# A decoder trunk on one core: first loads reordered, more warm-up matmuls, one PSUM tile moved, the last LayerNorm regrouped

## The chip, the core and the metric

The kernel runs on one core of one Trainium2 chip. The metric is the device time of one execution in microseconds (us). Beside it stands a profiled execution, whose trace gives the start and length of every instruction on five engines: TensorE (PE for matmuls, PEld for the weight loads that go ahead of them), VectorE (DVE), ScalarE (ACT), GpSimd (POOL) and SyncE (SP), and of the transfers on the core's 16 DMA engines.

## What is computed

One sequence of 256 tokens with 2048 features goes through two layers, all in float32:

```
for layer in (0, 1):
    shift, scale, gate = split(silu(c) @ ada_w[layer] + ada_b[layer], 3)
    h = x * (1 + scale) + shift
    y = ssd_mixer(h) if layer == 0 else dilated_attention(h, k, v)
    x = layer_norm(alpha * x + (1 + gate) * y) * ln_g[layer] + ln_b[layer]
    if layer == 0:
        k, v = split(x @ kv_w, 2)
```

The SSD mixer projects `h` to a gate z, to xs, B, C and dt, puts xs, B and C through a causal convolution of width 4, and forms for each of 8 groups a masked score matrix of C and B. The scores, weighted by decays, are multiplied with xs. The second layer is attention in three groups with dilated windows. The last step is a LayerNorm over 2048 features, times `ln_g`, plus `ln_b`.

## The kernel before

**Splitting.** Every large product runs in three passes. A weight piece `raw` (128 partitions x 1024 floats) is split by `split` (L97) into `whi`, a rounded copy made by ACT (L100), and `wlo`, the rest, made by DVE (L102); the activations are split in the same way. TensorE multiplies high by high, high by low and low by high (L151 to 153, L190 to 193, L224, L232 to 234).

**Order.** The program is written against a tile framework. It derives the semaphores from the data, and a list scheduler sets the order on each engine; `tc.issue_after` holds an instruction behind another one. An engine works its list strictly in order. A transfer uses one of eight semaphores in turn, so the ninth transfer waits at its issuing queue until the first has landed, and what stands behind it on that queue waits too.

**The start (L451 to 630).** `c` arrives as the small block `crow`; six warm-up matmuls of ones (`warm`, L457, two instructions each) run meanwhile. DVE splits `crow` (L466, L467), TensorE spreads it over all partitions in four tiles `cps` (L473), ACT makes silu(c) of each, `cb_` (L476), and 14 more warm-up matmuls follow. The shift and scale of a block of 128 features are each a dot product over a 1 MB block `araw` of `ada_w`: `fetch` (L483, through L310) loads one, DVE works it off in 2.3 us (L317; the first is cut in two halves, L501 and L503). From shift, scale and x^T (`xt`, loaded by `fetch_x`, L488) ACT makes `htmp` (L522) and `actT` (L524). The first three weight pieces come in half pieces (`begin_piece`, L558, and `end_piece`, L562); their first halves are multiplied unsplit (`plain`, L567, L575). The first loads are issued at L71 and L590 to L601, all on SP's queue but three: `c`, the bias block `adab` and the first `xt` go out on ACT's queue.

**The first SSD group.** `stage1(g)` (L739) multiplies B and C into the scores `pcb`, in a tile of the pool `aux`. That pool has two PSUM buffers, given out in turn; a buffer is handed on when its last reader is done. DVE masks the scores and copies them out (L748, L749). TensorE then transposes xs (L770) twice, for b = 0 and b = 1, each time into another `aux` tile; DVE makes `xd`, `y` and `xo` of them (L772, L775, L780). `stage2(g)` (L787) multiplies the weighted scores with `xd` into `py` (L803, pool `aux2`, also two buffers) and `cb` with `xo` into `po` (L792, `aux`). Meanwhile TensorE works on the products of the next group.

**The end (L1274 to 1346).** The block b = 1 is normalised last. Its mean comes from `bn_aggr` (L1289). For the column chunks 0 to 2, TensorE forms `u - mean * ln_g` in PSUM: `plus` (L1321) multiplies `u` by the identity, `centre` (L1325) adds `diag` times `ln_g`, where `diag` is the identity times minus the mean, made by DVE (L1328). Chunk 3 is centred by DVE itself (L1329). Meanwhile ACT takes a square root (L1290) and DVE refines the inverse root `r1` (L1293 to 1296). At last DVE multiplies each chunk by `r1` and adds `ln_b` (L1344), and SP stores it (L1272).

Of the kernel before, what the change touches and what calls it, by code (L numbers as in the profile page):

```python
# [9 lines left out]
F32 = mybir.dt.float32  # L10
# [3 lines left out]
ALU = mybir.AluOpType  # L14
# [35 lines left out]
def trunk(ctx, tc, xT, x, c, par, cst, bias, lnrow, ada, wdt, win, wxs, wout, wk, wv, wbin, wbout, out):  # L50
# [305 lines left out]
    with ExitStack() as cA:  # L356
# [15 lines left out]
        with ExitStack() as cS:  # L372
# [78 lines left out]
            with ExitStack() as c0:  # L451
# [9 lines left out]
                    return after  # L461

                at = mm.tile([P, 2, L], F32, name="acc")
                last = warm(6, at)
                crow2 = pe.tile([48, P + KT], F32R, name="crow", bufs=1)
                V.tensor_copy(crow2, crow)  # L466
                V.tensor_tensor(crow2[32:, :P], crow[32:, :P], crow2[32:, :P].bitcast(F32), op=ALU.subtract)  # L467
                with tc.tile_pool(name="ec", bufs=4, space=PSUM) as ec:
                    for n in range(4):
                        cps = ec.tile([P, 512], F32, name="cps")  # L470
                        for j in range(4):
                            with tc.issue_after(last.ins):
                                last = T.matmul(cps[:, j * P:j * P + P],  # L473
                                                crow2[:, P + 4 * n + j:P + 4 * n + j + 1].to_broadcast([48, P]),
                                                crow2[:, :P], start=True, stop=True)
                        S.activation(cb_[:, 512 * n:512 * n + 512], cps, AF.Silu)  # L476
                    last = warm(14, at, last)
                ex = c0.enter_context(tc.tile_pool(name="ex", bufs=4, space=PSUM))
                first = [acc_pair(ex), acc_pair(ex)]
                cols = [(0, kind, kt) for kt in range(KT) for kind in ("scale", "shift")]  # L480
# [2 lines left out]
                def fetch():  # L483
                    i = len(raws)
                    if i < len(cols):
                        raws.append(ada_load((wp1, pe)[i // 2 % 2], *cols[i]))

                def fetch_x(kt):  # L488
                    xts[kt // 2] = pe.tile([P, 2, L], F32, name="xt")
                    (nc.sync if kt else nc.scalar).dma_start(xts[kt // 2], xT[:, kt:kt + 2, :])  # L490

                def h_step():

# [94 lines left out]
                    halves[i] = [t.rearrange("p (k n) -> p k n", k=2) for t in halves[i]]  # L588

                nc.scalar.dma_start(adab_, par[:, :NB])  # L590
                fetch_x(0)
                fetch()
                fetch()
                begin_piece(0)
                begin_piece(1)
                fetch()
                fetch()
                begin_piece(2)
                for i in range(3):
# [139 lines left out]
            def stage1(g):  # L739

                pcb = aux.tile([P, 512], F32, name="aux")[:, :384].rearrange("p (a n) -> p a n", a=3)
                bm, cm_ = bc[g][:, 0, :], bc[g][:, 1, :]
                T.matmul(pcb[:, 0:3:2, :], bm[:, 0:P], cm_, start=True, stop=True)
                T.matmul(pcb[:, 1, :], bm[:, P:L], cm_[:, P:L], start=True, stop=True)
                cb = px.tile([P, 3, P], F32, name="cb")
                V.tensor_tensor(cb[:, 0:2, :], pcb[:, 0:2, :], tri[:, None, :].to_broadcast([P, 2, P]), op=ALU.mult)  # L748
                V.tensor_copy(cb[:, 2, :], pcb[:, 2, :])  # L749
                segs = []  # L750
                for w in range(2):
                    h0 = g * HPG + 4 * w
                    cbc = px.tile([P, 4, 2, P], F32, name="cbc")
                    nc.sync.dma_start(cbc, bass.AP(tensor=cumd.tensor, offset=cumd.offset + h0 * L,
                                                   ap=[[0, P], [L, 4], [P, 2], [1, P]]))
                    seg = px.tile([P, 4, 2, P], F32, name="seg")
                    for hh in range(4):
                        for b in range(2):
                            S.activation(seg[:, hh, b, :], cbc[:, hh, b, :], AF.Relu,  # L759
                                         bias=cumT[:, b, h0 + hh:h0 + hh + 1], scale=-1.0)  # L760
                    S.activation(seg, seg, AF.Exp, scale=-1.0)
                    V.tensor_tensor(seg.rearrange("p h b n -> p h (b n)"), seg.rearrange("p h b n -> p h (b n)"),
                                    cb[:, 0:2, :].rearrange("p b n -> p (b n)")[:, None, :].to_broadcast([P, 4, L]),
                                    op=ALU.mult)
                    segs.append(seg)
                xd = px.tile([P, 2, 512], F32, name="xd", bufs=1)
                for b in range(2):
                    px_ = aux.tile([P, 512], F32, name="aux")
                    for i in range(4):
                        T.transpose(px_[:, i * P:i * P + P], xs[g][:, i, b * P:b * P + P], ident)  # L770
                    heads = px_.rearrange("p (h e) -> p h e", h=HPG)
                    V.tensor_tensor(xd[:, b, :].rearrange("p (h e) -> p h e", h=HPG), heads,  # L772
                                    dtT[:, b, g * HPG:(g + 1) * HPG, None].to_broadcast([P, HPG, 64]),
                                    op=ALU.mult)
                    V.tensor_tensor(y[g][:, b, :].rearrange("p (h e) -> p h e", h=HPG), heads,  # L775
                                    dskip[:, g * HPG:(g + 1) * HPG, None].to_broadcast([P, HPG, 64]),
                                    op=ALU.mult)
                    if b == 0:
                        xo = px.tile([P, 512], F32, name="xo", bufs=1)
                        V.tensor_tensor(xo.rearrange("p (h e) -> p h e", h=HPG), heads,  # L780
                                        dec[:, 0, g * HPG:(g + 1) * HPG, None].to_broadcast([P, HPG, 64]),
                                        op=ALU.mult)
                return segs, xd, cb, xo
# [487 lines left out]
    def store(b, c):  # L1271
        nc.sync.dma_start(rows(out, b)[:, c], u[b][:, c])  # L1272

    diag = pc2.tile([P, 512], F32, name="sc0", bufs=1)[:, :P]  # L1274
    eps, sd = sm.tile([P, 1], F32, name="nm"), sm.tile([P, 1], F32, name="den")
    V.tensor_scalar(eps, ident[:, 0:1], 0.0, EPS, op0=ALU.mult, op1=ALU.add)
    with tc.issue_after(copied[-1].ins):
# [47 lines left out]
        return T.matmul(cen[n][:, cols], diag, lnt[:, 0, c], start=False, stop=True, skip_group_check=n == 2)  # L1325

    def between(mv):
        V.tensor_scalar(diag, ident, mv[:, 0:1], -1.0, op0=ALU.mult, op1=ALU.mult)  # L1328
        return V.scalar_tensor_tensor(u[1][:, chunk[3]], u[1][:, chunk[3]], mv[:, 0:1], lnt[:, 0, chunk[3]],  # L1329
                                      op0=ALU.subtract, op1=ALU.mult)  # L1330

    plus(1, plus(0, end))
    _, r1, step = root(1, between)
    centre(0)
    plus(2, centre(1))
    for h in range(2):
        centre(2, slice(256 * h, 256 * h + 256))
    for c in chunk:
        scaled(0, c)
        nc.gpsimd.dma_start(rows(out, 0)[:, c], u[0][:, c], accum_op=ALU.add)  # L1340
    for n, h0, h1 in ((0, 0, 512), (1, 0, 512), (3, 0, 512), (2, 0, 256), (2, 256, 512)):
        c = slice(512 * n + h0, 512 * n + h1)
        with tc.issue_after(step.ins):
            step = V.scalar_tensor_tensor(u[1][:, c], cen[n][:, h0:h1] if n < 3 else u[1][:, c], r1, lnt[:, 1, c],  # L1344
                                          op0=ALU.mult, op1=ALU.add)
        store(1, c)
# [95 lines left out]
```

## Time and profile before

| | |
|---|---|
| time, median of 3 runs | 1227.77 us (1227.69 to 1227.96) |
| the profiled execution's own time | 1229.04 us |
| its span, first to last instruction | 1227.2 us |
| DVE busy | 1018.4 us (83%) |
| ACT busy | 705.9 us (58%) |
| moved by DMA | 335.94 MB, mean 274 GB/s |
| granted TensorE clock | 1.000 |

The page of the profile gives each engine's busy time, the span cut in 40 slices, the chain of work that ended last, and the costliest groups of instructions. Timelines list the instructions of one engine with start and length; in square brackets stands the idle time before a row and what ended it. The view of windows gives busy time, number of instructions and GB/s for chosen stretches.

### The profile page before, as it was taken

To read this page: it belongs to the slowest core of one execution; us is meant where nothing else is said; L and a number is where in the kernel's file an instruction comes from. 1 tells how busy PE (TensorE), PEld (TensorE's weight loads), DVE (VectorE), ACT (ScalarE), POOL (GpSimd) and SP (SyncE) were. 2 spreads that over 40 slices of the span, in tenths; PEclk is the share of its full clock that TensorE was granted. 3 is DMA by queue.
4 is the path that set the end of the run, shared out by engine and by line. 5 is a ranking of instruction groups with operands and counts; after the bars stand their busy time and mean duration, and the time that the engine had idled before them with its cause. 6 is when DMAs were issued, how large, how long until landed. Compare 5 with 4: busy or idle time off the path is not lost.

```text
span 1227.2 us, 19061 instructions
## 1 busy us (share of the span) xinstructions
PE 1212.6 (99%) x7244; PEld 1039.9 (85%) x7244; DVE 1018.4 (83%) x1450; ACT 705.9 (58%) x1058; POOL 3.9 (0%) x8
## 2 busy tenths in 40 slices
PE   8999999999999999999999999999999999999998
PEld 8889998898888888778888888888888888888886
DVE  6989997899988889899778578888987885756886
ACT  4554567877597789764435455444435844444751
POOL 0000000000000000000000000000000000000001
PEclk9999999999999999999999999999999999999999
DMA  9999976686765556588988668989996885365673
GB/s 374 422 421 422 422 255 233 218 324 218 267 200 196 168 168 223 189 332 333 394 291 303 233 189 336 352 335 387 371 400 265 284 266 176 108 191 166 193 258 69
DMA packets 81372, 335.94 MB, mean 274 GB/s; under 512 B 9200, under 2 KB 9984, under 8 KB 68480
## 3 DMA queue, kind: packets, MB, share of 16 engines
q1 hardware_dynamic: 80352, 333.33, 75.0%
q0 software_dynamic: 576, 1.05, 0.6%
q8 instruction: 57, 0.93, 0.3%
q10 hardware_dynamic: 352, 0.34, 0.1%
q14 instruction: 35, 0.29, 0.1%
HBM read 331.45 MB, written 3.23 MB: 273 GB/s over the span
## 4 chain that ended last, share of the span: by engine, by line
PE 77%; DVE 10%; ACT 6%; DMA 5%; issue 2%; SPq 0%; DVEq 0%; ACTq 0%
PE acc L224 24%; PE acc L190 22%; PE acc L193 11%; DVE araw L317 4%; PE acc L233 3%; PE acc L234 3%; PE acc L232 3%; DVE wlo L102 3%; DMA raw<-in_win 2%; ACT whi L100 2%; PE py L803 1%; ACT seg L759 1%; DVE cacc L390 1%; DMA araw<-in_ada 1%; PE acc L153 1%
## 5 line engine op out<-in xcount | busy, mean ns | idle before, releaser
L100 ACT ACTIVATE whi<-raw 128x1024 fp32r<-128x1024 f32 x389 | 408.2, 1057 | 333.6 <-PE acc L190 110.3
L102 DVE TENSOR_TENSOR wlo<-raw,whi 128x1024 fp32r<-128x1024 f32 x389 | 469.2, 1219 | 139.8 <-ACT whi L100 134.0
L190 PE MATMUL acc<-actT,whi 128*128 128x512 f32 x1280 | 401.1, 394 | 0.0
L193 PEld LDWEIGHTS acc<-actT,wlo 128*128 128x128 f32 x1280 | 239.1, 188 | 53.4 <-DVE wlo L102 1.3
L193 PE MATMUL acc<-actT,wlo 128*128 128x256 f32 x1280 | 254.7, 280 | 0.6 <-DVE wlo L102 0.6
L317 DVE SCALAR_TENSOR_TENSOR araw<-araw,cb__72 128x2048 f32<-128x2048 f32 x95 | 216.8, 2283 | 2.9 <-DMA araw<-in_ada 2.7
L190 PEld LDWEIGHTS acc<-actT,whi 128*128 128x128 f32 x1280 | 194.8, 188 | 1.1 <-ACT whi L100 0.3
L224 PE MATMUL acc<-whi,actT 128*128 128x512 f32 x560 | 144.4, 392 | 0.5 <-ACT whi L100 0.5
L224 PEld LDWEIGHTS acc<-whi,actT 128*128 128x128 f32 x560 | 104.1, 188 | 22.0 <-ACT whi L100 0.9
L233 PE MATMUL acc<-wlo,actT 128*128 128x512 f32 x272 | 106.8, 393 | 1.3 <-DVE wlo L102 1.1
L151 PE MATMUL acc<-actT,whi 128*128 128x256 f32 x372 | 103.5, 282 | 1.4 <-ACT actT L524 1.1
L232 PE MATMUL acc<-whi,actT 128*128 128x512 f32 x272 | 104.6, 394 | 0.2 <-ACT sz L660 0.2
L224 PE MATMUL acc<-wlo,actT 128*128 128x512 f32 x384 | 103.5, 391 | 0.0
L153 PE MATMUL acc<-actT,wlo 128*128 128x256 f32 x372 | 101.9, 282 | 1.5 <-DVE wlo L102 1.5
L152 PE MATMUL acc<-actT,whi 128*128 128x256 f32 x372 | 103.1, 280 | 0.0
L234 PE MATMUL acc<-whi,actT 128*128 128x512 f32 x256 | 100.3, 392 | 0.0
L224 PEld LDWEIGHTS acc<-wlo,actT 128*128 128x128 f32 x384 | 71.6, 188 | 14.5
L151 PEld LDWEIGHTS acc<-actT,whi 128*128 128x128 f32 x372 | 69.5, 188 | 3.1 <-ACT actT L524 1.5
L152 PEld LDWEIGHTS acc<-actT,whi 128*128 128x128 f32 x372 | 70.8, 190 | 0.3
L153 PEld LDWEIGHTS acc<-actT,wlo 128*128 128x128 f32 x372 | 68.8, 188 | 2.4 <-DVE wlo L102 2.2
L233 PEld LDWEIGHTS acc<-wlo,actT 128*128 128x128 f32 x272 | 51.1, 188 | 12.6 <-DVE wlo L102 2.4
L232 PEld LDWEIGHTS acc<-whi,actT 128*128 128x128 f32 x272 | 50.8, 188 | 10.4 <-ACT sz L660 0.6
(321 smaller groups left out, 1298.2 us busy)
## 6 DMA issues: line engine op xcount, KB each, us to landing
araw<-in_ada SPq DMA_DIRECT2D x96, 1024.0 KB, 7.2
raw<-in_win SPq DMA_DIRECT2D x109, 512.0 KB, 6.3
raw<-in_wout SPq DMA_DIRECT2D x64, 512.0 KB, 5.7
raw<-in_wbin SPq DMA_DIRECT2D x64, 512.0 KB, 4.1
raw<-in_wxs SPq DMA_DIRECT2D x48, 512.0 KB, 4.5
raw<-in_wv SPq DMA_DIRECT2D x48, 512.0 KB, 6.7
raw<-in_wk SPq DMA_DIRECT2D x48, 512.0 KB, 7.7
cbc<-cumd SPq DMA_DIRECT2D x16, 512.0 KB, 5.2
```

Source lines behind the costliest of these rows:

```text
L100: copied.append(S.activation(hi, raw, AF.Copy))
L102: latest.append(V.tensor_tensor(lo, raw, hi.bitcast(F32), op=ALU.subtract))
L151: T.matmul(o, hi[:, k, c_], ahi[:, kt, :], start=first, stop=False, skip_group_check=True)
L152: T.matmul(o, hi[:, k, c_], alo[:, kt, :], start=False, stop=False, skip_group_check=True)
L153: T.matmul(o, lo[:, k, c_], ahi[:, kt, :], start=False, stop=kt == k1 - 1, skip_group_check=True)
L190: T.matmul(ps[n], hi[:, k, n * P:n * P + P], both(kt), start=kt == 0, stop=False, skip_group_check=True)
L193: T.matmul(ps[n][:, 0, :], lo[:, k, n * P:n * P + P], high(kt), start=False, stop=kt == KT - 1, skip_group_check=True)
L224: T.matmul(ps[b], a_(kt)[:, b * P:b * P + P], w_[:, k, :], start=a_ is ahi and w_ is hi and kt == k0, stop=w_ is lo and kt == k1 - 1)
L232: T.matmul(o, h_, hi[:, k, :], start=kt == k0, stop=False, skip_group_check=part)
L233: T.matmul(o, h_, lo[:, k, :], start=False, stop=False, skip_group_check=part)
L234: end = T.matmul(o, l_, hi[:, k, :], start=False, stop=kt == k1 - 1, skip_group_check=part)
L317: return V.scalar_tensor_tensor(raw, raw, 1.0, cb_, op0=ALU.mult, op1=ALU.mult, accum_out=mod[layer][:, ct, j:j + 1])
```

## The change

Four edits. The three early transfers on ACT's queue become two: the first `xt` is issued by SP, behind the first `araw`, and the third `araw` block is put ahead of the second half piece. The warm-ups grow from 6 to 11 ahead of the `cps` tiles and from 14 to 16 behind them. The scores of group 0 go to a tile of `aux2` (tag `py`) in place of `aux`. In the last LayerNorm, minus the identity is made ahead of time by DVE, `diag` is made from it by ACT, all three `plus` products are issued ahead of the `centre` products, and chunk 3 is the first to be scaled and stored.

```
-                last = warm(6, at)
+                last = warm(11, at)
...
-                    last = warm(14, at, last)
+                    last = warm(16, at, last)
...
-                    (nc.sync if kt else nc.scalar).dma_start(xts[kt // 2], xT[:, kt:kt + 2, :])
+                    nc.sync.dma_start(xts[kt // 2], xT[:, kt:kt + 2, :])
...
                 nc.scalar.dma_start(adab_, par[:, :NB])
+                fetch()
                 fetch_x(0)
                 fetch()
+                begin_piece(0)
                 fetch()
-                begin_piece(0)
                 begin_piece(1)
-                fetch()
                 fetch()
                 begin_piece(2)
...
-                pcb = aux.tile([P, 512], F32, name="aux")[:, :384].rearrange("p (a n) -> p a n", a=3)
+                pcb = aux2.tile([P, 512], F32, name="py") if g == 0 else aux.tile([P, 512], F32, name="aux")
+                pcb = pcb[:, :384].rearrange("p (a n) -> p a n", a=3)
...
-    diag = pc2.tile([P, 512], F32, name="sc0", bufs=1)[:, :P]
+    pair = pc2.tile([P, 512], F32, name="sc0", bufs=1)
+    diag, minus = pair[:, :P], pair[:, P:2 * P]
+    V.tensor_scalar(minus, ident, -1.0, None, op0=ALU.mult)
...
-        V.tensor_scalar(diag, ident, mv[:, 0:1], -1.0, op0=ALU.mult, op1=ALU.mult)
+        S.activation(diag, minus, AF.Copy, scale=mv[:, 0:1])
...
-    plus(1, plus(0, end))
+    plus(2, plus(1, plus(0, end)))
     _, r1, step = root(1, between)
     centre(0)
-    plus(2, centre(1))
+    centre(1)
...
-    for n, h0, h1 in ((0, 0, 512), (1, 0, 512), (3, 0, 512), (2, 0, 256), (2, 256, 512)):
+    for n, h0, h1 in ((3, 0, 512), (0, 0, 512), (1, 0, 512), (2, 0, 256), (2, 256, 512)):
```

## The prediction

> **What bounds the kernel now.** The page comes first:
>
> ```profile
> span 1227.2 us, 19061 instructions
> PE 1212.6 (99%) x7244; PEld 1039.9 (85%) x7244; DVE 1018.4 (83%) x1450; ACT 705.9 (58%) x1058; POOL 3.9 (0%) x8
> ```
>
> TensorE works 99% of the span, so only what starts it earlier, fills one of its gaps or shortens the tail can count: 1227.2 - 1212.6 = 14.6 us idle in all. But busy isn't useful at the start, where warm-ups are counted. The view of windows shows what rules there (columns: window and its length, then busy time and instructions of PE, PEld, DVE, ACT and POOL, granted clock, DMA share, GB/s):
>
> ```profile
> 7.00:11.00 4.00, 4.00 (x19) 3.88 (x19) 2.68 (x5) 1.79 (x3) 0.00 (x0) 1.00 0.98 324
> 11.00:15.00 4.00, 4.00 (x24) 3.92 (x24) 2.73 (x6) 1.02 (x2) 0.00 (x0) 1.00 1.01 424
> 15.00:20.00 5.00, 4.73 (x21) 3.53 (x20) 4.96 (x7) 1.48 (x3) 0.00 (x0) 1.00 1.04 410
> 30.00:155.00 125.00, 123.16 (x816) 112.05 (x815) 116.17 (x125) 65.40 (x85) 0.00 (x0) 1.00 1.02 422
> ```
>
> From 7 to 155 us the DMA engines have hardly an idle share, so weights come as fast as they can, and whatever transfer time is lost early moves everything to 155 us. TensorE is nearly full there too, so it can't make up for lateness later. One window stands out: 324 GB/s from 7 to 11 us.
>
> The gaps that the change aims at stand in the timelines of PE, DVE and PEld, in order of time:
>
> ```profile
> 1.09 2.93 PE L460 MATMUL acc<-ones 128*128 128x128 f32 x12 [1.09 <-DVE ones L455]
> 5.21 3.67 PE L473 MATMUL cps<-crow 48*128 48x128 f32 x16 [1.19 <-DVE crow L467]
> 8.81 5.51 PE L460 MATMUL acc<-ones 128*128 128x128 f32 x28
> 14.16 5.57 PE L575 MATMUL acc<-htmp,raw 128*128 128x256 f32 x24
> 20.78 0.39 PE L151 MATMUL acc<-actT,whi 128*128 128x256 f32 x1 [1.05 <-ACT actT L524]
> 9.55 1.23 DVE L503 SCALAR_TENSOR_TENSOR araw<-araw,cb__72 128x1024 f32<-128x1024 f32 x1 [0.47 <-ACT cb__72 L476]
> 13.21 0.16 DVE L322 TENSOR_TENSOR mod<-mod,adab 128x2 f32<-128x2 f32 x1
> 14.60 2.29 DVE L317 SCALAR_TENSOR_TENSOR araw<-araw,cb__72 128x2048 f32<-128x2048 f32 x1 [1.23 <-DMA araw<-in_ada]
> 17.16 2.28 DVE L317 SCALAR_TENSOR_TENSOR araw<-araw,cb__72 128x2048 f32<-128x2048 f32 x1
> 230.10 0.63 PE L770 MATMUL aux<-cc,xs 128*128 128x128 f32 x4 [1.87 <-DVE cb L749]
> 1219.48 0.30 PEld L1325 LDWEIGHTS aux<-actT,sc 128*128 128x128 f32 x2 [0.73 <-DVE sc L1328]
> ```
>
> DVE waits 1.23 us for the third `araw`; TensorE waits 1.87 us at 228 us and once more in the tail.
>
> **Part 1, the loads.** In the slow window ACT's queue (q10) works off the first `xt` beside the half pieces on SP's queue (q1). The view of the DMA of 7 to 11 us:
>
> ```profile
> q1 hardware_dynamic: 342, 1.02, 70.0%
> q10 hardware_dynamic: 202, 0.28, 28.1%
> ```
>
> Short packets alone don't do it: the four later half pieces go out in 15 to 20 us, on SP's queue only, at 410 GB/s. I therefore take the mix of two queues as the cause. Loss: 4 us x (424 - 324) / 424 = 0.94 us. With `xt` on SP's queue I count this as won, for every later load, as DMA never idles again before 155 us. The bounds: 0 (the rate stays) and 1.23 us (DVE's whole wait for the load behind the window, if the slowest of the 16 engines loses more than the mean); I take the mean of the window.
>
> Besides, the third `araw` no longer stands behind a half piece of 0.26 MB: 0.26 / 0.42 = 0.62 us more for it alone, given back by that half piece. So it lands 1.56 us before 14.6, at 13.0. DVE is free at 13.21 + 0.16 = 13.37 and starts there, 1.2 us earlier; the fourth, now read at 17.16, lands 0.94 us earlier and bounds what follows: 0.94, not 1.2. The cost on SP is one issue more ahead of the second `araw` (timeline of SP, then its waits):
>
> ```profile
> 0.74 0.86 SPq L310 DMA_DIRECT2D araw<-in_ada  x2
> SPq L563 <- DMA xt<-in_xT: 2.5, 1, 2.5
> ```
>
> That is 0.86 / 2 = 0.43 us, hidden by the first block's own 1 MB (2.5 us at 422 GB/s); uncovered it would cost 0.43. The second `araw` lands some 0.6 us later, but DVE comes to it only behind L503, at 10.78. The wait of 2.5 us in the last row, the eighth semaphore turn taken by `xt`, goes; behind it stand two end pieces and later loads, yet the engines had work all that time, so this wins nothing, and what of it is uncovered is in the 1.23 above.
>
> By the Trainium skill ("DMA: Bandwidth & Descriptors", section "Issuing engines are not separate DMA queues") transfers from all queues share 16 engines, and a second queue saves issue time only; the rows above speak against it, 324 beside 410 to 424 GB/s. If it held, the sum would lose the 0.94: that is rival C.
>
> **Part 2, the warm-ups.** Two instructions make one warm-up. The price of a narrow matmul at two times:
>
> ```profile
> 9.40:13.20 3.80, 3.80 (x19) 3.80 (x19) 1.00 1.00 389
> 13.40:14.10 0.70, 0.70 (x9) 0.70 (x7) 1.00 1.00 421
> ```
>
> (windows of L460 alone; columns PE, PEld, clock, DMA, GB/s). Before 13.3 us one takes 3.80 / 18 = 0.21 us (19 touch the window, one of them in part), afterwards 0.70 / 7 = 0.10 by the weight loads, though the granted clock stands at 1.00. ACT's last silu ahead of L503 is
>
> ```profile
> 8.92 0.60 ACT L476 ACTIVATE cb__72<-cps 128x512 f32<-128x512 f32 x1 [0.26 <-PE cps L473]
> ```
>
> The faster pace came about 4.5 us into the unbroken run from 8.81. Five more warm-ups are 10 x 0.21 = 2.1 us: TensorE, free of the first ones near 3.8, comes to `cps` at 5.95, not 5.21, a delay of 0.74, but now in a run unbroken since 1.09, so the pace should change near 5.6 and the 16 `cps` matmuls take about 1.8 in place of 3.5. Then ACT's four silus of 0.6 set the pace and the last ends near 9.3, against 8.92 + 0.60 = 9.52. Bounds: 0.47 us won (DVE's wait at 9.55) and 0.74 lost (pace unchanged). What hides either is the wait for the loads: 1.23 us at 14.60 as things are, the fourth `araw` afterwards. I take 0; uncovered it would be these bounds. The later two warm-ups (0.4 us) end before `htmp` lets L575 start.
>
> **Part 3, the scores' tile.** The stall of 1.87 us goes: the second transposes no longer wait for the scores' readers. What is late next? The view of windows, then the timelines of DVE and PE:
>
> ```profile
> 224.20:246.90 22.70, 20.83 (x147) 16.49 (x146) 22.65 (x36) 17.41 (x33) 0.00 (x0) 1.00 0.57 193
> 233.33 0.68 DVE L772 TENSOR_TENSOR xd<-aux,dtT 128x512 f32<-128x512 f32 x1
> 235.31 0.68 DVE L780 TENSOR_TENSOR xo<-aux,dec 128x512 f32<-128x512 f32 x1
> 235.24 1.15 PE L803 MATMUL py<-xd,seg 128*64 128x64 f32 x30
> 236.31 1.12 PE L792 MATMUL aux<-xo,cb 128*128 128x512 f32 x2
> ```
>
> DVE works 22.65 of 22.70 us; it never waited for those transposes. Its times stay, and TensorE reaches L803 near 233.4 and waits: `xd` is done at 234.0, `xo` at 235.99. L792 can start at 236.04 in place of 236.31. So 0.27 us of the 1.87 are kept and 1.6 become a new wait one step later. Bounds: 0, and 1.9 if the scheduler finds other work. I take 0.27. The tile borrowed from `aux2` costs nothing: its last reader, L749, is done before L770 starts at 230.10, and `py` needs it only behind L803's first half.
>
> **Part 4, the tail.** The timelines of PE, DVE and ACT, and a window:
>
> ```profile
> 1217.70 1.88 PE L1321 MATMUL aux<-u,cc 128*128 128x512 f32 x4
> 1219.48 1.98 PE L1325 MATMUL aux<-actT,sc 128*128 128x512 f32 x4
> 1221.30 1.02 PE L1321 MATMUL po<-u,cc 128*128 128x512 f32 x2
> 1222.16 1.03 PE L1325 MATMUL po<-actT,sc 128*128 128x256 f32 x4
> 1219.20 0.29 ACT L1290 ACTIVATE den<-e1mv,nm 128x1 f32<-128x1 f32 x1 [6.22 <-DVE e1mv L1289]
> 1223.22 0.88 DVE L1344 SCALAR_TENSOR_TENSOR u<-po,e1y,actT 128x256 f32<-128x256 f32 x2 [0.31 <-PE po L1325]
> 1219.14 0.29 DVE L1328 TENSOR_SCALAR sc<-cc,e1mv 128x128 f32<-128x128 f32 x1
> 184.06 0.31 ACT L713 ACTIVATE araw<-araw 128x128 f32<-128x128 f32 x1
> 1192.76 1.28 ACT L1278 ACT_TABLE_LOAD   x1
> 1210.05 2.93 ACT L1307 ACTIVATE u<-u,e0nb,e0y 128x512 f32<-128x512 f32 x4 [0.88 <-DVE e0nb L1305]
> 1195.00:1212.00 17.00, 17.00 (x77) 14.08 (x76) 10.82 (x23) 2.25 (x4) 0.00 (x0) 1.00 0.00 0
> ```
>
> The end hangs on TensorE's last product: DVE waits 0.31 us for it, scales two halves and stores. A wide product starts (1.88 - 1.02) / 2 = 0.43 us behind the last. With all `plus` ahead the run is 1217.70 + 10 x 0.43 = 1222.0, where the last four begin, against 1222.16: 0.16 to 0.2 us earlier, as `diag` is no longer awaited. `diag` on ACT stands behind the square root, at 1219.5, and a 128x128 ACTIVATE takes 0.31 (L713): ready at 1219.85, before TensorE needs it at 1220.27. On DVE L1328's 0.29 goes, and chunk 3, scaled first, fills the wait for `centre`. Making `minus` is one more such instruction near 1190; hidden by TensorE's full run behind it, in which DVE is busy 10.82 of 17.00 us (uncovered: 0.29). I take 0.2; bounds 0 and 0.4. If ACT had to load a table for the copy, as at L1278 (1.28 us), `diag` would be ready at 1221.1 and the tail 0.8 longer; but L1307 runs behind block 0's square root without a load in its row.
>
> **Sum.** 0.94 + 0 + 0.27 + 0.2 = 1.4 us. The profiled execution would go from 1229.04 (span 1227.2 and 1.84 around it) to 1227.6; it lies 1.27 above the median. From the median: 1227.77 - 1.4 = **1226.4 us**.
>
> **Rivals.**
> B, the stall is kept as a gain: other TensorE work fills the wait, 0.94 + 1.9 + 0.2 = 3.0, giving 1224.7. For it: TensorE is 99% busy. Against: DVE has no slack until 246.9.
> C, the queues don't matter: the slow window has another cause and stays; 0.27 + 0.2, giving 1227.3. For it: the half pieces go out in the same window.
> D, TensorE slows again. The quick `cps` let the warm-ups end near 11.8, and L575 starts near 14: 2.2 us idle, where the longest idle that the quick pace is seen to survive is 1.05 (before 20.78). If it falls back, the 24 instructions of L575 take 0.43 and not 5.57 / 24 = 0.22 each (with the end's drain): for 4.5 us, 10 of them, +2.2, for all of them +5.2, so L151 starts between 21.4 and 24.3, and TensorE, full afterwards, is 0.6 to 3.5 us late; less parts 3 and 4, 0.47, this gives 1227.9 to 1230.8, middle 1229.3. It decides as soon as the idle is too long. By the Trainium skill ("TensorE: Matmul & The Clock Gate", Part 1) the full clock comes after about 3.4 us of work and goes after as long a window without; by it D falls away, and no row here has such an idle.
>
> **Chances.** Forecast 55% (1225.6 to 1227.0), B 13%, C 22%, D 6%, an order remade elsewhere to unknown effect 4%. A measurement tells about 0.2% (2.5 us) from no change. Faster by more: B and the forecast's lower tail, 0.20. Slower: half of D and of the rest, 0.06. Range 1224.4 to 1228.0: it holds B and C and leaves most of D out.
>
> **What would show it.** Part 1: no idle before the third L317, 410 GB/s or more in 7 to 11 us, L151 first near 19.8. Part 2: `cps` from 5.95 at half the spacing. Part 3: L770 without a wait, a new wait of about 1.6 us before L803 or L792. Part 4: the last four L1325 at 1222.0 on the old scale. Wrong if the window stays slow, or if TensorE shows no new wait near 234 us.

## The result, and the profile after

The changed kernel is slower: 1233.12 us, median of 6 runs (1230.21 to 1233.69), against 1227.87 us for the kernel before in runs beside it (6 runs, 1226.81 to 1228.71). The ratio is 1.0039, with a 95% interval of 1.0026 to 1.0052, so the whole interval lies above the 0.2% that a measurement can tell. The forecast was 1226.4 us, the range 1224.4 to 1228.0.

The profiled execution took 1233.69 us. Its page:

```profile
span 1231.9 us, 19090 instructions
...
PE 1217.2 (99%) x7258; PEld 1044.5 (85%) x7258; DVE 1019.3 (83%) x1450; ACT 704.8 (57%) x1057; POOL 3.9 (0%) x8
...
PEclk9999999899999999999999999999999999999999
```

TensorE is again busy for 99% of the span, but 4.6 us longer than before (1217.2 against 1212.6) for the same products and 7 more warm-ups. The third row, the granted clock in 40 slices, tells where: one slice stands at 8, in which before has 9 throughout. A slice is 1231.9 / 40 = 30.8 us, so the clock fell between 215.6 and 246.4 us, in the first group of the SSD.

To place a loss, the 392 splits of weights on ACT (L100, `whi` from `raw`) can be matched between two traces by number, as every kernel here makes the same ones. From about 40 to 206 us the changed kernel is 0.7 us ahead. By 400 us it is 3.9 us behind, and 4.9 behind at the last split. So 4.6 us are lost between 206 and 400 us; another 1.0 us goes in small steps between 500 and 1200 us, which wasn't traced. The view of windows between two such splits (number 69 and number 130, counted from 0, the same work in both), first before, then after:

```profile
206.16:396.56 190.40, 188.53 (x1324) 164.49 (x1323) 172.05 (x283) 149.49 (x252) 0.00 (x0) 1.00 0.68 236
```

```profile
205.46:400.44 194.98, 191.07 (x1320) 166.18 (x1319) 170.98 (x281) 147.31 (x251) 0.00 (x0) 0.98 0.68 230
```

The stretch grew by 4.58 us. TensorE's busy time grew by 191.07 - 188.53 = 2.54, as the same products ran for a while at half clock, and its idle time from 1.87 to 3.91, by 2.04. These are the two halves of the loss in this execution. The idle half stands in the view of TensorE's waits from 205 to 275 us, where before has only the 1.87 us at L770:

```profile
PE py L804 <- DVE xd L773: 1.8, 1, 1.8
PE aux L793 <- DVE xo L781: 1.3, 1, 1.3
```

Before, the stall stood ahead of the second transposes; now there are two, one each ahead of the products of `xd` and `xo`, and they lie close together. The other half stands in the windows that follow the clock's own record: it shows half clock from 232.58 us for 6.827 us, and full clock otherwise from 14.12 us to the end.

```profile
229.16:232.58 3.42, 1.15 (x32) 1.01 (x32) 3.42 (x9) 3.04 (x6) 0.00 (x0) 1.00 0.00 0
232.58:235.99 3.41, 2.61 (x14) 1.14 (x16) 3.41 (x7) 1.14 (x3) 0.00 (x0) 0.50 0.02 5
235.99:239.41 3.42, 3.42 (x31) 2.92 (x28) 3.42 (x4) 2.87 (x10) 0.00 (x0) 0.50 0.52 153
```

In the 3.42 us ahead of the fall TensorE worked 1.15 us. In the kernel before, the stretch that holds the stall of 1.87 us had

```profile
228.32:231.73 3.41, 1.62 (x10) 1.44 (x11) 3.41 (x8) 2.83 (x5) 0.00 (x0) 1.00 0.59 241
```

and the clock stayed.

Why are there two waits, and why so long? The order of instructions was remade when the tile changed. TensorE's order in the two programs (`z`, `xs`: products of L232 to L234 and L151 to L153; L770 and L771 are the transposes, L803 and L804 the products of `xd`, L792 and L793 that of `xo`):

```
before  64 z, L726, L727, 4 z, 2 L735, 13 z, 144 xs, scores L745 L746,
        4 L770, 18 z, 4 L770, 20 z, 15 L803, L792, 17 L803, 4 xs, 34 z
after   35 z, scores L746 L747, 35 z, L726, L727, 3 z, 2 L735, 8 z, 144 xs,
        8 L771, 26 z, 16 L804, L793, 16 L804, 46 z
```

With a tile of `aux2` the scores need no buffer of `aux`, and they stand some 30 us earlier (193.3 us in the trace, 222.9 before); everything around them moved too. Between the transposes and the products of `xd` there are now 26 products of z instead of 38. The timeline of DVE in the changed kernel, and one row of ACT:

```profile
199.34 0.42 DVE L749 TENSOR_TENSOR cb<-py,cc 128x256 f32<-128x256 f32 x1
...
203.09 1.23 DVE L102 TENSOR_TENSOR wlo<-raw,whi 128x1024 fp32r<-128x1024 f32 x1
...
217.40 1.23 DVE L102 TENSOR_TENSOR wlo<-raw,whi 128x1024 fp32r<-128x1024 f32 x1 [4.09 <-DMA raw<-in_win]
...
223.94 1.23 DVE L102 TENSOR_TENSOR wlo<-raw,whi 128x1024 fp32r<-128x1024 f32 x1 [1.77 <-ACT whi L100]
...
230.17 0.68 DVE L773 TENSOR_TENSOR xd<-aux,dtT 128x512 f32<-128x512 f32 x1
...
232.55 0.68 DVE L781 TENSOR_TENSOR xo<-aux,dec 128x512 f32<-128x512 f32 x1
...
234.53 1.22 DVE L102 TENSOR_TENSOR wlo<-raw,whi 128x1024 fp32r<-128x1024 f32 x1
```

```profile
224.76 1.99 ACT L100 ACTIVATE whi<-raw 128x1024 fp32r<-128x1024 f32 x2
```

`cb` is made at 199.34, where before it came at 226.59. `xd` is done at 230.85, 3.2 us earlier than before (234.01), but TensorE has waited for it since 229.13 (its product starts at 230.91 after 1.78 us idle). The 12 products of z that no longer stand between are just one piece of weights (two blocks of 128 features, two halves of the tokens, three passes). The windows of L102 alone, from 205 to 229 us (length, DVE's busy time and number, clock, DMA share, GB/s), before and then after, show DVE splitting fewer pieces:

```profile
205.00:229.00 24.00, 8.56 (x7) 1.00 0.80 277
```

```profile
205.00:229.00 24.00, 6.12 (x5) 1.00 0.80 267
```

Five instead of seven, but one of the two was only done earlier, ahead of the window (203.09; its counterpart before starts at 206.03). Counted from the start, DVE has split 75 pieces by 229 us before, 74 after, and 75 again in scores_held, below. The missing piece was rounded by ACT at 225.81 (the first of the two in the row of ACT), but its split on DVE, at 234.53, now stands behind the convolution, `xd` and `xo`; before, the 75th split was done at 225.47. So this piece is held by DVE's order. The loads may have a part in it: SP issues these weights in turn with the `cbc` loads, and in the new order the `cbc` loads of the next pair wait there for their buffers, with weights behind them (view of SP's waits from 190 to 246 us; before has no such row). Which of the moved instructions pushed the piece back wasn't separated.

```profile
SPq L755 <- ACT seg L760: 6.5, 2, 3.4
```

### The profile page after: what moved, and what is told of

It reads as the page before. It is cut to its first block, busy times and chain, and to the rows that moved or that the text cites. A ratio compares the mean times of both kernels' runs of the same rounds, so it can differ in the third digit from the quotient of the medians.

```text
span 1231.9 us, 19090 instructions
## 1 busy us (share of the span) xinstructions
PE 1217.2 (99%) x7258; PEld 1044.5 (85%) x7258; DVE 1019.3 (83%) x1450; ACT 704.8 (57%) x1057; POOL 3.9 (0%) x8
## 4 chain that ended last, share of the span: by engine, by line
PE 76%; DVE 11%; ACT 6%; DMA 5%; issue 2%; SPq 0%; DVEq 0%; ACTq 0%
PE acc L224 23%; PE acc L190 20%; PE acc L193 10%; PE acc L233 4%; DVE araw L317 4%; PE acc L234 3%; PE acc L232 3%; DVE wlo L102 3%; DMA raw<-in_win 3%; ACT whi L100 2%; PE acc L153 1%; PE acc L151 1%; PE acc L152 1%; DVE cacc L390 1%; ACT seg L760 1%
## 5 line engine op out<-in xcount | busy, mean ns | idle before, releaser
L100 ACT ACTIVATE whi<-raw 128x1024 fp32r<-128x1024 f32 x389 | 408.7, 1057 | 344.2 <-PE acc L190 111.6
L102 DVE TENSOR_TENSOR wlo<-raw,whi 128x1024 fp32r<-128x1024 f32 x389 | 469.7, 1221 | 136.6 <-ACT whi L100 128.3
L193 PEld LDWEIGHTS acc<-actT,wlo 128*128 128x128 f32 x1280 | 239.0, 188 | 54.4 <-DVE wlo L102 2.5
L193 PE MATMUL acc<-actT,wlo 128*128 128x256 f32 x1280 | 254.7, 280 | 1.4 <-DVE wlo L102 1.4
L232 PE MATMUL acc<-whi,actT 128*128 128x512 f32 x272 | 104.5, 394 | 0.1
L153 PE MATMUL acc<-actT,wlo 128*128 128x256 f32 x372 | 102.2, 282 | 1.7 <-DVE wlo L102 1.7
L151 PE MATMUL acc<-actT,whi 128*128 128x256 f32 x372 | 103.3, 281 | 0.0
L234 PE MATMUL acc<-whi,actT 128*128 128x512 f32 x256 | 100.8, 394 | 0.0
L153 PEld LDWEIGHTS acc<-actT,wlo 128*128 128x128 f32 x372 | 68.8, 188 | 2.7 <-DVE wlo L102 2.6
L151 PEld LDWEIGHTS acc<-actT,whi 128*128 128x128 f32 x372 | 69.7, 188 | 0.8 <-ACT s L660 0.2
L233 PEld LDWEIGHTS acc<-wlo,actT 128*128 128x128 f32 x272 | 51.5, 189 | 13.3 <-DVE wlo L102 3.0
L232 PEld LDWEIGHTS acc<-whi,actT 128*128 128x128 f32 x272 | 51.0, 188 | 10.5 <-ACT sz L660 0.6
```

What stands on the lines that cost most here:

```text
L100: copied.append(S.activation(hi, raw, AF.Copy))
L102: latest.append(V.tensor_tensor(lo, raw, hi.bitcast(F32), op=ALU.subtract))
L151: T.matmul(o, hi[:, k, c_], ahi[:, kt, :], start=first, stop=False, skip_group_check=True)
L153: T.matmul(o, lo[:, k, c_], ahi[:, kt, :], start=False, stop=kt == k1 - 1, skip_group_check=True)
L193: T.matmul(ps[n][:, 0, :], lo[:, k, n * P:n * P + P], high(kt), start=False, stop=kt == KT - 1, skip_group_check=True)
L232: T.matmul(o, h_, hi[:, k, :], start=kt == k0, stop=False, skip_group_check=part)
```

## The experiments

The theory: the whole loss comes from the scores' tile, by the order that was remade around it; half is waits, half is the half clock that they bring on. Rivals: the loads or the warm-ups lose the time; the tile itself costs it, whatever the order; the clock fell for another reason. The times, with the median of the kernel before on the same chip (0.9 to 1.3 us over the 1227.77 from which most expectations start, so what counts is the difference):

| kernel | median us (runs) | before us | ratio, 95% interval |
|---|---|---|---|
| no_scores | 1227.82 (12) | 1229.03 | 0.9990, 0.9980 to 1.0000 |
| scores_only | 1233.27 (6) | 1229.03 | 1.0032, 1.0020 to 1.0045 |
| scores_held | 1229.00 (11) | 1229.03 | 0.9999, 0.9991 to 1.0008 |
| loads_tail | 1228.12 (12) | 1229.03 | 0.9995, 0.9985 to 1.0005 |
| fill | 1232.25 (7) | 1228.69 | 1.0036, 1.0022 to 1.0050 |
| best | 1227.78 (11) | 1228.69 | 0.9994, 0.9985 to 1.0003 |
| xt_act | 1234.32 (4) | 1228.69 | 1.0041, 1.0026 to 1.0055 |
| warm_only | 1228.73 (1) | 1228.69 | one run |
| fill4 | 1232.40 (5) | 1228.98 | 1.0034, 1.0022 to 1.0047 |
| fill1 | 1233.86 (5) | 1228.98 | 1.0039, 1.0025 to 1.0052 |

### no_scores: the change without the tile

```
-                pcb = aux2.tile([P, 512], F32, name="py") if g == 0 else aux.tile([P, 512], F32, name="aux")
-                pcb = pcb[:, :384].rearrange("p (a n) -> p a n", a=3)
+                pcb = aux.tile([P, 512], F32, name="aux")[:, :384].rearrange("p (a n) -> p a n", a=3)
```

> The changed kernel with the scores of the first SSD group back in a tile of the pool aux; the loads, the warm-ups and the end stay changed. Theory (the whole loss comes from the scores' tile, by an order of instructions that was remade around it): 1227.77 - 0.7 (the lead that the splits on ScalarE hold from 18 to 206 us) - 0.2 (the tail) = 1226.9 us, and no stretch of half clock near 235 us. Rival 1 (the loads or the warm-ups lose the time): 1230 us or more, with the half clock still there. Rival 2 (the tile costs its two waits, 1.8 + 1.3 us, and the half clock comes from elsewhere): about 1230 us, half clock still there.

Measured: 1227.82 us beside 1229.03, full clock from 6.3 us to the end. Three parts of the four gain 1.2 us together by the medians (the interval reaches from 0 to 2.5 us); the loss is gone with the fourth. The first rival falls, and so does the second one of the expectation, as there is no half clock without the tile.

### scores_only: the tile alone

The two lines above, the other way round, in the kernel before.

> The kernel before with the scores' tile alone changed. Theory: the loss of the changed kernel without its gains, 1227.8 + 4.6 = 1232.4 us (between 1230 and 1234), TensorE waits twice near 230 us, one stretch of half clock follows, and the scores' products stand some 20 us earlier in TensorE's order than before. Rival 1 (loads or warm-ups lose the time): 1227.5 to 1227.8, as the prediction had it for this part alone.

Measured: 1233.27 us, 4.2 over the kernel before. The waits are the same two, 2.5 and 1.3 us, and the clock's record shows half clock for 6.827 us from 233.40. The tile alone brings a loss of this size.

### scores_held: the tile, but the order of before

```
+                with tc.issue_after(cm_end[-1].ins) if g == 0 else ExitStack():
+                    T.matmul(pcb[:, 0:3:2, :], bm[:, 0:P], cm_, start=True, stop=True)
```

on scores_only. `cm_end` keeps the last product of C of the piece before, so the scores can't run ahead of it. TensorE's and SP's orders are then those of the kernel before; on DVE and ACT a few neighbours near 230 us change places.

> The kernel before with the scores in a tile of aux2, but their products held behind the last product of C, where they stand in the kernel before. If the order does the harm and not the tile: no half clock, TensorE's stall of 1.87 us before the transposes gone, a new wait of about 1.6 us before the products of xd or xo, 1227.5 us (the prediction's 0.27 us), within 1226 to 1228. If the tile alone does it: two waits and the half clock as in the changed kernel, 1230 to 1234.

Measured: 1229.00 us, the same as before (1229.03 beside it), though above the 1226 to 1228 that was expected. TensorE's waits from 210 to 250 us in its trace:

```profile
PE py L805 <- DVE xd L774: 0.8, 1, 0.8
PE aux L794 <- DVE xo L782: 0.5, 1, 0.5
```

The stall of 1.87 us is gone, 1.3 us of it came back one step later, and the clock stays full there. Windows between the same two splits as above:

```profile
206.18:395.92 189.74, 188.43 (x1324) 164.59 (x1323) 172.06 (x283) 149.36 (x252) 0.00 (x0) 1.00 0.68 237
```

190.40 - 189.74 = 0.66 us gained. So it is the order that does the harm; with the order kept, the tile does in the trace about what the prediction's part 3 said, and a little more, and nothing that the medians show.

### loads_tail: the loads and the end, without the warm-ups

```
-                last = warm(11, at)
+                last = warm(6, at)
...
-                    last = warm(16, at, last)
+                    last = warm(14, at, last)
```

on no_scores.

> The changed kernel with the scores' tile and both counts of warm-ups (6 and 14) as before: the loads and the end alone. By the prediction's terms 1227.77 - 0.94 - 0.2 = 1226.6 us, with the first product with weights from whi at 19.8 us of the trace. If the five more warm-ups delay the scores' way into ScalarE by the 0.74 us that was the prediction's bound and that shows, this is some 0.2 to 0.7 us faster than the same kernel with the new warm-ups; if they cost nothing, the two are equal. Rival C of the prediction (the queues don't matter): 1227.5, first product at 20.7.

Measured: 1228.12 us, within 0.3 of no_scores: the warm-ups cost and win nothing that shows. The first product with `whi` starts at 20.12 in both traces to 0.02 us (20.78 before), not at 19.8 and not at 20.7. Its trace holds a second fall of the clock, far from the change, behind a wait of 1.84 us for `wlo`:

```profile
983.83:987.25 3.42, 1.58 (x10) 1.07 (x9) 3.30 (x4) 1.06 (x1) 0.00 (x0) 1.00 0.88 259
987.25:990.66 3.41, 3.41 (x13) 2.93 (x12) 3.41 (x6) 0.61 (x1) 0.00 (x0) 0.50 0.89 338
```

### fill, fill4 and fill1: work in the wait

Dummy products of constants stand between the 26 products of z and the first of `xd`, in the tile that these overwrite (`5` is 4 and 1 in the other two):

```
+                    py0 = aux2.tile([P, 512], F32, name="py")
+                    fill(py0, 5, tm_ends[base[0] + 2])
...
+                        after = T.matmul(at[:, :P], ones, ident, start=True, stop=True)
```

> The changed kernel with five dummy products of the constants (128x128, f32, results overwritten) on TensorE between its 26 products of z and the first products of xd, held there; nothing else changes its place on TensorE. They fill 5 x 0.2 = 1.0 us of the wait of 1.8 us. Theory (of the 4.6 us lost, 3.4 are half of the 6.83 us at half clock, which follow because TensorE worked only 1.15 of the 3.42 us from 229.16 to 232.58; the other 1.2 are the two waits of 3.1 us in place of one of 1.87): with 1.0 us of work more that stretch holds at least 2.1 us, above the 1.62 us that the kernel before had in one such stretch without a drop, so no half clock and 1233.1 - 3.4 = 1229.7 us. Rival (the clock falls for another reason, or costs nothing because TensorE waits then anyway): 1233 us again, with or without the half clock.

Measured: no half clock in its trace near 235 us, but 1232.25 us, with runs from 1229.90 to 1235.97. With five dummies a few neighbours had changed places on the other engines, so the comparison isn't clean. The next two keep every engine's order as in the changed kernel.

> The changed kernel with four of the dummy products in the wait before the first products of xd (0.8 of its 1.8 us); with four, unlike five, the order of every engine stays exactly that of the changed kernel. Stretches of 3.41 us seen so far: TensorE busy 1.15, 1.31, 1.42 and 1.58 us, half clock in the next; 1.62, 2.10, 2.28 and 2.60 us, none. With 0.8 us more the worst stretch holds about 1.15 + 0.8 = 1.95 us: no half clock near 235 us in the trace and in most runs, and the time is the changed kernel's less 3.4 us, 1229.7 (1229 to 1231). Rival (the waits alone are the loss, the clock falls beside them without cost or for another reason): 1233 us.

> The control: the same code with one dummy product (0.2 us), the same order on every engine. The worst stretch holds about 1.35 us of work, under the 1.58 us with which the clock fell: half clock for 6.83 us as in the changed kernel, 1232 to 1234 us in most runs, 3 us over the kernel with four. If the dummies act in another way than by the clock (the order, the tile kept busy), the two kernels are equal.

Measured: 1232.40 us with four and 1233.86 with one, with ranges that overlap (1231.47 to 1235.01 and 1230.66 to 1234.99), so the times alone don't tell the two apart; four had been expected at 1229 to 1231. The mean clock was 0.999 or more in 4 of 5 runs with four, and in 1 of 5 with one. The timeline of TensorE and the two stretches of the clock's grid in fill4, then two of fill1:

```profile
229.02 1.05 PE L794 MATMUL py<-cc 128*128 128x128 f32 x8
231.40 1.15 PE L802 MATMUL py<-xd,seg 128*64 128x64 f32 x32 [1.32 <-DVE xd L774]
233.87 1.10 PE L817 MATMUL aux<-xo,cb 128*128 128x512 f32 x2 [1.32 <-DVE xo L782]
```

```profile
228.78:232.19 3.41, 2.09 (x36) 1.84 (x36) 3.41 (x8) 3.03 (x5) 0.00 (x0) 1.00 0.02 6
232.19:235.61 3.42, 2.10 (x40) 1.24 (x36) 3.42 (x8) 2.02 (x4) 0.00 (x0) 1.00 0.00 0
```

```profile
230.06:233.47 3.41, 1.15 (x32) 1.01 (x32) 3.41 (x9) 3.20 (x5) 0.00 (x0) 1.00 0.00 0
233.47:236.88 3.41, 2.79 (x18) 1.32 (x19) 3.41 (x6) 0.97 (x3) 0.00 (x0) 0.50 0.02 5
```

So the traces bear the mechanism out: `xd` comes no earlier, TensorE does no more useful work, and yet 2.1 us of work in the stretch in place of 1.15 keep the clock. Sorted afterwards by clock, the five of these ten runs with 0.999 or more (room for one stretch of 3.41 us at half clock at most) have a median of 1232.01 us, the other five 1234.58, 2.6 us apart. (The mean clock counts a fall anywhere in the execution.) The same sorting of the changed kernel's six runs gives 1230.21, 1231.96 and 1232.68 us with 0.999 or more, and 1233.55 to 1233.69 below: only half of them have the 6.8 us of half clock, and the others still lose 2 to 5 us. The price of the fall was smaller than expected. Between the same two splits fill4 has

```profile
206.16:398.63 192.47, 188.78 (x1328) 164.85 (x1327) 170.59 (x281) 147.28 (x250) 0.00 (x0) 1.00 0.68 233
```

that is 194.98 - 192.47 = 2.51 us less than the changed kernel, not 3.4, and 2.07 more than before. Half of 6.83 us would be lost only if TensorE had been the bound all through it; it was busy for 2.61 + 3.42 = 6.03 us of them, so 3.0 us at most; where the other half microsecond went wasn't traced. The medians show less still, 1.5 us between fill4 and fill1, because fill4 gives some back late: against the changed kernel its splits are 1.8 us ahead up to 860 us and 0.3 us from 990 us on. In that stage its waits of L193 for `wlo` add up to more than in the kernel before (views of TensorE's waits over the span, before and then fill4):

```profile
PE acc L193 <- DVE wlo L102: 0.6, 1, 0.6
```

```profile
PE acc L193 <- DVE wlo L102: 2.9, 3, 1.7
```

Over the twelve traces this row goes from 0.5 to 2.9 us, with the change and without it. What sets it stays open.

### best: the change, with the scores held

The edit of scores_held in the changed kernel.

> The changed kernel with the scores' products held behind the last product of C, so loads, warm-ups and end as changed, the tile as changed, the order as before. By the parts alone: 1227.8 (the changed kernel without the tile) - 0.5 (what the held tile gains from 235 us on in the trace of the kernel with that alone) = 1227.3 us. It also has no wait over 1 us near 230 us, and so should have fewer runs with a clock below 0.999 than the kernel before. If the tile's gain is eaten by the next wait: 1227.8.

Measured: 1227.78 us beside 1228.69, no better than no_scores by its median; its profiled span, 1225.1 us, is the shortest of all traces, and its longest wait near 230 us is 0.2 us. In that trace the way from 191 to 244 us gains 1.8 us on the kernel before, in no_scores 0.5: without the waits the held tile is worth about 1.3 us there, but the medians neither show nor exclude it. Of 11 runs one has a clock under 0.999; of the 18 runs of the kernel before, two, which shows no difference. Its trace has a fall of the clock at the start instead. Timeline of TensorE, and the windows:

```profile
13.71 7.13 PE L575 MATMUL acc<-htmp,raw 128*128 128x256 f32 x24 [2.40 <-ACT htmp L522]
20.49 0.82 PE L151 MATMUL acc<-actT,whi 128*128 128x256 f32 x4
```

```profile
11.70:15.12 3.42, 1.42 (x7) 1.26 (x8) 2.95 (x6) 1.02 (x2) 0.00 (x0) 1.00 1.02 418
15.12:18.53 3.41, 3.41 (x10) 2.70 (x9) 2.84 (x4) 0.63 (x1) 0.00 (x0) 0.50 1.02 398
```

### xt_act: the new order of loads, `xt` on ACT's queue

```
-                    nc.sync.dma_start(xts[kt // 2], xT[:, kt:kt + 2, :])
+                    (nc.sync if kt else nc.scalar).dma_start(xts[kt // 2], xT[:, kt:kt + 2, :])
```

> The changed kernel with the first load of xT back on ScalarE's queue, its other loads in the new order. The rate over the eight microseconds from 3 to 11 us is what counts: before 416 and 324 GB/s, after 350 and 413, so the slow stretch moved ahead rather than went. If the mix of two queues makes it (the prediction's part 1): 324 to 350 GB/s in one of the two halves and 10 to 30 GB/s less in the other than after has, the sum of both below after's 763 and near before's 740. If it is the loads' short pieces on whichever queue (its rival C): the sum is after's 763 within 5. Time: that of the changed kernel (1230 to 1234), as the scores are left as changed.

Measured: both answers miss. Windows of its start:

```profile
3.00:7.00 4.00, 4.00 (x31) 3.82 (x30) 0.51 (x2) 1.46 (x4) 0.00 (x0) 1.00 1.03 423
7.00:11.00 4.00, 4.00 (x35) 3.77 (x34) 3.92 (x5) 1.03 (x3) 0.00 (x0) 1.00 0.97 359
```

The sum is 782, over all others. In this trace two queues at once don't lower the rate over the whole start. The order around it changed too: `htmp` came late and TensorE waited 5.58 us for it, so the time, 1234.32, says nothing about the queue.

### warm_only: the warm-ups alone

The two counts of loads_tail, the other way round, in the kernel before.

> The kernel before with the 22 and 32 warm-up instructions alone. Theory, from six traces: the full clock is granted at the end of a fixed stretch of 3.41 us in which TensorE worked nearly throughout on full products; the 16 products of 48 rows don't count. With 5.06 us of warm-ups from 1.09 us on, half of the executions hold such a stretch before those products (grant at 4.5 to 6.15 us, then 2.1 us for them), the others get it only behind them (grant from 13 us on, then 3.7 us for them); nothing between. Either way the first product with weights of whi starts within 0.5 us of the 20.78 us of the kernel before, and the time is the same, 1227 to 1230 us. The prediction's part 2 (quick from 5.6 us in every execution) has 1.8 us for them and nothing else.

Measured: 1228.73 us beside 1228.69. The clock was granted at 4.40 us, slightly ahead of the expected 4.5 to 6.15; the sixteen products took 2.0 us, and the first product with `whi` started at 20.45:

```profile
5.30 2.00 PE L473 MATMUL cps<-crow 48*128 48x128 f32 x16
```

## Why the prediction was wrong, point by point

**Part 3 failed, and with it the sum.** The step is "DVE works 22.65 of 22.70 us; it never waited for those transposes. Its times stay". They didn't: `xd` came 3.2 us earlier, TensorE 4.3 us earlier (229.13) than the 233.4 that the step gave it, with one piece of weights less. The prediction read the change as one wait taken away in a fixed order, while the order is made anew by a scheduler that sees which buffer is free. It said that the tile "costs nothing" and gave 0 as the lower bound. That no instruction waits longer for the tile is right; that none moves because of it was never asked. "An order remade elsewhere to unknown effect" had 4% and no place. With the order held the step is nearly right: 0.27 us expected, 0.66 in the trace and 0.03 by the medians, with a new wait of 1.3 us (0.8 and 0.5) where 1.6 was forecast, at the two instructions named.

**Rival D's mechanism came true at another place.** The prediction asked whether the clock survives an idle time of 2.2 us at the start, and gave 6%. It didn't ask the same of the new wait that part 3 itself forecast at 234 us. At the start it happened too (best: 7.13 us for L575; 5.34 to 6.67 in the ten traces without a fall there), but the first `whi` product came at 20.49 us, and at 20.12 to 20.46 in the five other traces with the same start, so it cost 0.4 us at most, where D had 0.6 to 3.5. The prediction put beside D the Trainium skill ("TensorE: Matmul & The Clock Gate", Part 1), read as saying that the full clock goes only after a whole idle window of 3.4 us, by which D falls away. The runs agree with its length of 3.413 us and with the stretches being fixed in time, not begun by the work; they don't agree with that reading, since 1.58 us of work in the stretch didn't hold the clock.

**Part 1: the cause was wrong, and the size isn't shown.** The forecast was 0.94 us, from a slow DMA stretch that would go. The changed kernel's windows:

```profile
3.00:7.00 4.00, 4.00 (x20) 3.77 (x19) 0.51 (x2) 0.00 (x0) 0.00 (x0) 1.00 0.96 350
7.00:11.00 4.00, 4.00 (x19) 3.88 (x20) 1.81 (x3) 2.39 (x4) 0.00 (x0) 1.00 1.02 413
```

From 7 to 11 us the rate is 413 as forecast, but from 3 to 7 it fell to 350, from

```profile
3.00:7.00 4.00, 2.81 (x14) 2.51 (x13) 0.51 (x2) 1.03 (x2) 0.00 (x0) 1.00 1.00 416
```

before. The slow stretch moved ahead with `xt`. Over the first 30 us the DMA engines moved 11.18 MB before and 11.24 after, a difference of 0.06 MB or 0.14 us at 422 GB/s. Rival C was right that the queue doesn't matter. Whether the new order of loads wins something all the same stays open: the changed kernel is 0.7 us ahead from 40 to 206 us, no_scores 0.6, loads_tail 0.5 to 1.0, but of the traces with the old loads scores_only is 0.9 ahead in most of that stretch, and only scores_held and warm_only are not ahead. What can be followed is DVE's own chain:

```profile
10.42 1.23 DVE L503 SCALAR_TENSOR_TENSOR araw<-araw,cb__72 128x1024 f32<-128x1024 f32 x1 [0.47 <-ACT cb__72 L476]
...
14.15 2.29 DVE L317 SCALAR_TENSOR_TENSOR araw<-araw,cb__72 128x2048 f32<-128x2048 f32 x1
...
16.70 2.29 DVE L317 SCALAR_TENSOR_TENSOR araw<-araw,cb__72 128x2048 f32<-128x2048 f32 x1
```

The wait for the third `araw` is gone, as forecast, and the fourth is read at 16.70 instead of 17.16. The third landed near 13.1 (loads_tail reads it at 13.07 after a wait), as the forecast 13.0 had it. So 0.46 us was won at this step, and the first `whi` product came at 20.46 and not at 19.8. The rest of the lead wasn't traced to a step.

**Part 2: the time was right, the reason wrong.** Zero was forecast, with the 16 `cps` products quick from 5.6 us on. In the changed kernel they are slow:

```profile
1.09 5.06 PE L460 MATMUL acc<-ones 128*128 128x128 f32 x22 [1.09 <-DVE ones L455]
6.08 3.67 PE L473 MATMUL cps<-crow 48*128 48x128 f32 x16
...
15.46 5.35 PE L575 MATMUL acc<-htmp,raw 128*128 128x256 f32 x24
```

So the upper bound of 0.74 came true at L503, 0.87 late (10.42 against 9.55), and the cover named for it held: DVE reached the third `araw` after it had landed, and nothing was lost. In no_scores, with the same start, the clock was granted at 6.29 us and the 16 products took 2.09 us, so their pace is a matter of the execution. The pace doesn't come some 4.5 us into a run of work. Before 13.28 us the trace of before has no record of the clock at all, and the views print 1.00 for that; the prediction took this as a clock granted and looked for another cause of the pace.

**Part 4: right.** Forecast 0.2 us. From the last split of weights on ACT to the end of the span it is 35.5 us in the four traces with the old end (35.48 to 35.50) and 35.3 in the eight with the new one (35.31 to 35.33). The end in the changed kernel:

```profile
1225.18 1.88 PE L1328 MATMUL aux<-actT,sc 128*128 128x512 f32 x4
1226.90 1.03 PE L1328 MATMUL po<-actT,sc 128*128 128x256 f32 x4
```

The last four start 4.29 us behind the first `plus` (1222.61); on the old scale that is 1217.70 + 4.29 = 1221.99, and 1222.0 was forecast. The copy of `diag` took 0.39 us, not 0.31, and no table was loaded.

Without part 3 the sum is 0.94 + 0.2 = 1.1, and no_scores gained 1.2 by its median. With an interval from 0 to 2.5 us, and part 1's cause wrong, this agreement may be luck.

## What to carry to other kernels

Where a scheduler makes the order, an edit that frees a buffer is an edit of the order: hold the instruction where it was (one edge, as in scores_held) or compare the order of every engine before pricing the wait that goes. Cost an idle time on TensorE by what it leaves of work in a stretch of 3.41 us: two waits of 1.8 and 1.3 us close together cost more than both lengths, through the clock. A dip of the DMA rate in one window is a loss only if the bytes moved by a later time are fewer.

## What the runs showed of the hardware

The granted clock changes on a grid of 3.413 us: the stretches of half clock in the twelve traces, apart from their ends, last 3.413 or 6.827 us. Where the grid lies differs from one execution to the next, so that the same program can fall in one run and not in another. What decides, as far as these traces show, is TensorE's busy time in one stretch of the grid, at full clock:

| busy in the stretch of 3.41 us | kernel and place | next stretch |
|---|---|---|
| 0.00 | xt_act, 11 us | half |
| 1.15 | changed kernel, scores_only and fill1, near 231 us | half |
| 1.31 | xt_act, 231 us | half |
| 1.42 | best, 13 us | half |
| 1.58 | loads_tail, 985 us | half |
| 1.59 | fill1, 13 us | full |
| 1.62 | before, 230 us | full |
| 2.09, 2.10 | fill4, near 230 and 234 us | full |

From 1.65 up to 2.75 us stand 37 more stretches in the twelve traces that kept the clock, so the border here is about 1.6 us, just under half, and the kernel before runs close to it. It isn't sharp: in the last microseconds of the program, left out above, a stretch with 1.52 us (scores_only, from 1226.68 us) kept the clock, and one with 1.36 (fill1) lost it. There are two exceptions, both at the start: 2.41 us in loads_tail and 2.96 in scores_only, and the clock fell. Both hold the 16 `cps` products of 48 rows (2.0 us) behind an idle time of 1.2 and 1.14 us, so these seem to count for little. To come back took more than to stay: at half clock 2.61 us of work (the changed kernel, from 232.58 us), and up to 2.84 in scores_only, weren't enough, and in all nine cases in which the clock came back the stretch was full, 3.41 us. But the first grant came behind 2.73 us in scores_only and 2.93 in loads_tail, all of it warm-ups, so a full stretch isn't always needed.

The first grant came at 4.2 to 6.9 us in nine of the twelve traces, and at 13.3 to 14.1 in before, the changed kernel and scores_held, behind the products of 48 rows, though in the changed kernel TensorE had worked without a gap since 1.09 us.
